# Chunk preparation of a gated DeltaNet: the decay matrix from matmuls, or from cumulative sums read back by DMA

## The chip, the cores and the metric

The kernel runs on one core of one Trainium2 chip. The time is device microseconds of one execution. Three runs of the kernel before gave 1589.02, 1593.64 and 1592.56 us, so the median is 1592.56 us. The profile is of a further execution, which took 1596.21 us.

## The reference

One layer (DEPTH is 1) works on 1024 latent tokens and 256 context tokens of width 1024, all in float32. An input projection, fed by RMS norm and modulation, feeds two groups: a gated DeltaNet with 4 heads of 128 and a neighbourhood attention with 8 heads of 64. An output projection and a SwiGLU feed-forward layer (width 2816) follow. What matters here is the DeltaNet, which is scanned forward and backward over the 1280 tokens in chunks:

```
qkv = short_conv(p[..., :3 * DN_WIDTH], conv_w)          # centred, 5 taps, SiLU
g   = -exp(A_log) * softplus(a + dt_bias);  beta = sigmoid(b)
gam = cumsum(g) inside a chunk
decay = exp(where(tril, gam[:, None] - gam[None, :], -inf))
m   = where(strict, (k * beta) @ k.T * decay, 0);  a_mat = I + m
u, w: triangular solves with a_mat;   qk = where(tril, q @ k.T * decay, 0)
scan over the chunks: v_new = u - w S;  o = q exp(gam) S + qk v_new;  S = S exp(g_last) + k_dec.T v_new
```

For each chunk and direction the kernel needs the decay matrix (the exponential of differences of cumulative sums, zero on the wrong side of the diagonal), the masked product of the keys times that matrix, and the inverse of a_mat. All of this can be done before the scan begins.

## The kernel before, in words

**Tiling.** The kernel works with chunks of 128 tokens: NCH = 10 chunks (2 of context, 8 of latent tokens), 2 directions, 4 heads. That makes 20 preparations, each for the four heads of one chunk and direction, in tiles of 128 partitions by 4 x 128 float32 (256 KB).

**Order of the work.** All engines' instruction streams are written by one Python program, and each engine runs its own stream in that order. The projection is a list `jobs` (line 952): blocks of 128 output columns (`Block`: k, q, v of the DeltaNet, nk, nq of the attention) and wide pieces (`Wide`: z and nv). The loop of line 974 does job n's matmuls (`j.mm`, line 389, three split products of float32r at a time; `wide`, line 572), steps background generators between them (`bg.step`), evacuates the bank (`evac`), and then does the norm of job n - 1 and the `finish` of job n - 2 (transposes and products of k with k and q with k).

**The convolution.** For q and v blocks `evac` copies the bank into a tile `cr` and puts the whole convolution on VectorE behind it at the end of the job: for each of the two segments (context, latent) one multiplication (line 441) and four multiply-adds (line 445), so ten instructions for v and five for q; `silu` (line 452, ScalarE) follows directly.

**The background.** `bg` holds two generators. `block_inverses` makes the decay tables (`decay_tables`, line 711: G, the cumulative exponentials EG, KD, ET) and then the inverses of the 32 x 32 diagonal blocks. Its end (lines 841 to 847) transposes the blocks and stores both forms in HBM as `x_d`. `preps` (line 853) makes the 20 preparations: at most three are alive at a time, each steps in turn, and a preparation takes seven steps. The four context preparations can run early; the 16 latent ones wait until the q blocks are finished (line 935). From then on `bg.step(3)` stands behind each of the eight row groups of a block, and `bg.step(5)` behind each tile of a wide piece (lines 1007, 1013). `bg.drain()` (line 984) completes them ahead of the last job.

**One preparation** (`prep`, line 879), with its steps separated by `yield`:

1. GpSimd multiplies the two halves of g (GH, GL, a high and a low float32r part) by a triangular mask into `rg` (line 886, two instructions); ScalarE and GpSimd spread the loaded blocks `xc` into `fx` (line 891) and `y` (line 892).
2. TensorE makes the differences of cumulative sums by three matmuls into one bank: two of `rg` against a mask (line 896) and one that adds -1e30 on the wrong side (line 897). ScalarE takes the exponential from PSUM into `e` (line 900). VectorE multiplies `kk` by e and by -beta, head by head (line 902, four instructions), and for latent chunks `at` by e (line 905); `at` is stored.
3. TensorE multiplies by the diagonal inverses (line 911, four matmuls), ScalarE evacuates (line 913).
4. to 6. Three rounds of small matmuls (line 920), each evacuated by VectorE (line 921). The result `y` is stored two ticks later.

Loads of a preparation (`fetch`, line 868: `kk`, `xc` and for latent chunks `at`) and all stores are issued on the SP queue, in the order of the program. A fetch is issued when no other fetched chunk is waiting. Buffers: kk 4, xc 3, at 3, e 2, rg 2, y 6.

**Around it.** Weights of the next job are loaded on SP at the start of a job, cast on ScalarE (line 198) and their low half is made on GpSimd (lines 199, 565). The convolution's early blocks (k) use another path (line 431). Behind the projections come the scan together with the attention, the output projection and the feed-forward layer, which read `y_d` and `at_d` from HBM.

## Time and profile before

| What | Value |
|---|---|
| Median of three runs | 1592.56 us (1589.02 to 1593.64) |
| The profiled execution | 1596.21 us, span of its instructions 1594.4 us |
| Busy share of the span: TensorE, its weight loads, VectorE, ScalarE, GpSimd | 93%, 78%, 64%, 45%, 13% |
| Granted TensorE clock, mean | 0.979 |
| DMA, mean over the span | 173 GB/s |
| Context preparations | about 295 to 336 us |
| Latent preparations | about 427 to 570 us |
| Scan and attention | about 600 to 850 us |

The span is the time from the first instruction to the last; a run's time is 1.8 us longer. "Busy" of TensorE is a union of modelled spans: consecutive matmuls overlap in it, so the distance from one start to the next tells more than a duration. Rows of groups give the count, the busy time, the mean duration of one instruction, and the engine's idle time ahead of them with what ended it.

### The profile page before, as it was taken

The numbers are of one execution on the slowest core, as the hardware profiler recorded it, in microseconds if no ns is written. First come the engines' busy times: TensorE is split into PE (matmuls) and PEld (weight loads), VectorE is DVE, ScalarE is ACT, GpSimd is POOL, SyncE is SP. The second block draws the span as 40 slices with busy tenths as digits, with TensorE's granted clock in tenths as the row PEclk, the third lists the DMA queues.
The fourth block names the chain that finished last, engine by engine and source line by source line (L and its number), as shares of the span: only waits on it lengthen the run. The fifth ranks groups of instructions, "written<-read, shape, count | busy, mean of one in ns | idle before, by whom it ended". The sixth has DMA issues, their size and how long they took to land.

```text
span 1594.4 us, 23945 instructions
## 1 busy us (share of the span) xinstructions
PE 1489.2 (93%) x8594; PEld 1239.2 (78%) x8594; DVE 1019.4 (64%) x1934; ACT 711.0 (45%) x1348; POOL 206.2 (13%) x278
## 2 busy tenths in 40 slices
PE   3999999899989997998897999999999999999999
PEld 1689788678978776887775877888888888888887
DVE  5866678335365565778886558866665555689652
ACT  5343362754435335666663246333333333545441
POOL 2044610532254200000000000000000000000000
PEclk9999999999999999999998999999999999999999
DMA  9457123444446369999737710623333333798742
GB/s 369 122 187 226 57 80 133 168 128 145 163 145 212 110 176 297 278 272 279 242 101 250 245 40 27 198 101 111 100 116 108 113 107 105 229 376 296 254 152 86
DMA packets 211528, 275.23 MB, mean 173 GB/s; under 512 B 15952, under 2 KB 119888, under 8 KB 210384
## 3 DMA queue, kind: packets, MB, share of 16 engines
q1 hardware_dynamic: 210544, 273.06, 53.1%
q8 instruction: 68, 1.11, 0.3%
q10 hardware_dynamic: 864, 0.63, 0.1%
q14 instruction: 52, 0.43, 0.1%
HBM read 206.78 MB, written 71.04 MB: 174 GB/s over the span
## 4 chain that ended last, share of the span: by engine, by line
PE 74%; DVE 7%; DMA 7%; ACT 6%; issue 3%; POOL 2%; SPq 1%; ACTq 0%; DVEq 0%; POOLq 0%
PE ps L1218 26%; PE ps L1565 13%; PE blk L389 11%; PE blk L572 4%; PE ps L1349 4%; PE sc L317 2%; PE pr L920 2%; PE sc L307 2%; PE sc L295 1%; PE ps L1111 1%; DVE tt L824 1%; PE ps L1371 1%; DMA fraw<-w_conv 1%; PE pr L911 1%; PE ps L1128 1%
## 5 line engine op out<-in xcount | busy, mean ns | idle before, releaser
L389 PE MATMUL blk<-hh,whi 128*128 128x512 f32 (+1 forms) x416 | 127.3, 399 | 4.1 <-ACT whi L198 1.6
L389 PE MATMUL blk<-hh,wlo 128*128 128x512 f32 (+1 forms) x416 | 120.8, 385 | 2.3 <-POOL wlo L199 2.3
L1279 ACT CAST uhi<-ws 128x512 fp32r<-128x512 f32 x91 | 54.7, 623 | 150.8 <-PE ps L1218 76.4
L1279 ACT CAST uhi<-wq 128x512 fp32r<-128x512 f32 x101 | 60.6, 621 | 137.0 <-issue 61.3
L389 PE MATMUL blk<-hl,whi 128*128 128x512 f32 (+1 forms) x416 | 119.2, 380 | 0.0
L1280 DVE TENSOR_TENSOR ulo<-wq,uhi 128x512 fp32r<-128x512 f32 x101 | 67.6, 688 | 68.3 <-ACT uhi L1279 37.2
L1218 PE MATMUL ps<-hT,uhi 128*128 128x512 f32 x336 | 104.7, 393 | 3.1 <-ACT hT L1397 3.1
L1218 PE MATMUL ps<-hT,ulo 128*128 128x512 f32 x336 | 103.9, 390 | 0.0
L1218 PE MATMUL ps<-lT,uhi 128*128 128x512 f32 x336 | 103.9, 391 | 0.0
L389 PEld LDWEIGHTS blk<-hh,wlo 128*128 128x128 f32 x416 | 75.3, 197 | 19.2 <-POOL wlo L199 2.9
L1218 PE MATMUL ps<-hB,uhi 128*128 128x512 f32 x288 | 89.7, 392 | 0.0
L1218 PE MATMUL ps<-lB,uhi 128*128 128x512 f32 x288 | 89.2, 391 | 0.0
L1218 PE MATMUL ps<-hB,ulo 128*128 128x512 f32 x288 | 89.1, 390 | 0.0
L389 PEld LDWEIGHTS blk<-hh,whi 128*128 128x128 f32 x416 | 72.2, 197 | 20.3 <-issue 3.0
L572 PE MATMUL blk<-zhi,hh 128*128 128x264 f32 (+1 forms) x288 | 85.2, 296 | 0.4 <-ACT kk L534 0.4
L389 PEld LDWEIGHTS blk<-hl,whi 128*128 128x128 f32 x416 | 74.4, 194 | 14.1
L1280 DVE TENSOR_TENSOR ulo<-ws,uhi 128x512 fp32r<-128x512 f32 x91 | 60.8, 686 | 37.3 <-ACT uhi L1279 29.0
L572 PE MATMUL blk<-zhi,hl 128*128 128x264 f32 (+1 forms) x288 | 83.4, 290 | 0.0
L572 PE MATMUL blk<-zlo,hh 128*128 128x264 f32 (+1 forms) x288 | 82.7, 287 | 0.0
L1218 PEld LDWEIGHTS ps<-hT,uhi 128*128 128x128 f32 x336 | 63.4, 189 | 16.6 <-ACT hT L1397 3.5
L1218 PEld LDWEIGHTS ps<-hT,ulo 128*128 128x128 f32 x336 | 63.4, 189 | 13.2
L1218 PEld LDWEIGHTS ps<-lT,uhi 128*128 128x128 f32 x336 | 63.4, 189 | 13.2
(331 smaller groups left out, 3614.9 us busy)
## 6 DMA issues: line engine op xcount, KB each, us to landing
wq<-w_fo SPq DMA_DIRECT2D x99, 256.0 KB
wq<-w_gu SPq DMA_DIRECT2D x88, 256.0 KB
wad<-wa SPq DMA_DIRECT2D x64, 256.0 KB
bt<-rpb SPq DMA_DIRECT2D x64, 192.0 KB
t_d<-g SPq DMA_DIRECT2D x22, 512.0 KB
fr<-t_d SPq DMA_DIRECT2D x44, 256.0 KB
f_d<-g SPq DMA_DIRECT2D x33, 256.0 KB
fr<-f_d SPq DMA_DIRECT2D x33, 256.0 KB
```

The source lines that it names most:

```text
L295: pe.matmul(sc[:, u * 640 + n0:u * 640 + n1], q, ks[i], start=i == 0, stop=i == 1)
L307: pe.transpose(sc[:, u * 640 + j * 128:u * 640 + (j + 1) * 128], bt[:, j * 128:(j + 1) * 128], ident)
L317: pe.matmul(sc[u * ND:u * ND + ND, 1280:1408], vv, pt[:, j * 128:(j + 1) * 128], start=j == 0, stop=j == 4)
L389: pe.matmul(o, ww[:, k], xx[k][:, s], start=k == 0 and j == 0, stop=k == KT - 1 and j == end)
L572: pe.matmul(p[:, :c1 - c0], x[k][:, s], ww[:, k, c0:c1], start=k == 0 and j == 0, stop=k == KT - 1 and j == 2)
L824: dve.tensor_tensor(t, N[:P, :, 0:c, c:c + 1].to_broadcast([P, 4, c, w]), N[:P, :, c:c + 1, c + 1:32].to_broadcast([P, 4, c, w]), OP.mult)
L920: pe.matmul(p[q, h * 128:h * 128 + 32 * r], f[:, h, q], y[:, h, s], start=True, stop=True)
L1218: pe.matmul(o, w[wi][:, k], x[xi][:, k], start=first and k == 0 and j == 0, stop=k == n - 1 and j == 2, skip_group_check=True)
L1279: act.copy(hi, self.raw[key])
L1280: dve.tensor_tensor(lo, self.raw[key], hi.bitcast(F32), OP.subtract)
L1349: pe.matmul(o, w[wi][:, k], parts[xi][k][:, s], start=k == 0 and j == 0, stop=k == KT - 1 and j == 2)
L1565: pe.matmul(o[b], w[wi][:, b], F[xn, p][xi], start=n in (0, 1, 5) and p == 0 and j == 0, stop=p == NFB // 2 - 1 and j == 2, skip_group_che ...
```

## The change

Three things change in the preparation, and two in what feeds it.

- **Decay matrix.** `decay_tables` keeps the negated cumulative sums `GN` (partition = token), transposes them once on TensorE, and stores the sums as 80 rows of 128 in HBM (`g_d`); G is clamped from below at -110. `fetch` loads the four rows of a chunk into every partition of `e` (a read of 2 KB repeated for 128 partitions). GpSimd sets the wrong side of the diagonal to -1e30 with `affine_select` (in place of the two products into `rg`), and ScalarE makes the exponential with the partition's own -sum as bias, head by head (four instructions from SBUF in place of one from PSUM). The three matmuls and their masks `mr[4]` and `mneg` are gone.
- **Beta.** -beta (`NB`) is multiplied into the stored diagonal inverses (two VectorE products of 128 x 1280 in `block_inverses`), so that `kk` is multiplied by e in one VectorE instruction and not in four.
- **Loads.** Up to two fetched chunks wait ahead of the running ones. Buffers: kk 5, xc 4, at 4, e 4 (now filled by the load), y 4.
- **Convolution.** The ten (or five) VectorE instructions of a block become a generator `taps`, stepped during the next job: two per row group of a block, three per tile of a wide piece; `silu` comes at its end.
- One `yield` is added in `decay_tables`, so everything behind it in `bg` is one step later.

```diff
@@ -135,8 +135,7 @@
     for i, v in enumerate((EPS, -0.5 * math.log(64.0))):
         dve.memset(bias[:, i:i + 1], v)
     b_eps, b_naq = bias[:, 0:1], bias[:, 1:2]
-    mr = const("mr", [128, 5, 128], F32R)
-    mneg = const("mneg", [128, 2, 128], F32R)
+    mr = const("mr", [128, 4, 128], F32R)
 
     v_d = dram.tile([T, 512], F32, name="v_d", tag="v_d")
     k_d = dram.tile([T, 512], F32, name="k_d", tag="k_d")
@@ -153,6 +152,7 @@
     y_d = dram.tile([2, NCH, 128, 4, 128], F32, name="y_d", tag="y_d")
     at_d = dram.tile([2, 8, 128, 4, 128], F32, name="at_d", tag="at_d")
     x_d = dram.tile([128, 2, 2, NU, 32], F32, name="x_d", tag="x_d")
+    g_d = dram.tile([2 * NU, 128], F32, name="g_d", tag="g_d")
     x2_d = dram.tile([KT, 128, L], F32, name="x2_d", tag="x2_d")
     f_d = dram.tile([NFB, 2, 128, 512], F32, name="f_d", tag="f_d")
     t_d = dram.tile([NFB, 2, 128, 512], F32, name="t_d", tag="t_d")
@@ -173,6 +173,7 @@
     EG = const("EG", [128, 2, NCH, 4])
     KD = const("KD", [128, 2, NCH, 4])
     ET = const("ET", [128, 2, NCH, 4])
+    GN = const("GN", [128, 2, NCH, 4])
     act.activation(sc2, c2, AF.Silu)
     bg = Background()
 
@@ -435,16 +436,24 @@
                 raw = cp.tile([128, T], F32, name="cr", tag="cr", bufs=2)
                 for p, s0, n in self.pss:
                     act.copy(raw[:, s0:s0 + n], p[:, :n])
+                self.later = self.taps(raw, acc, blk)
+
+            later = None
+
+            def taps(self, raw, acc, blk):
                 for lo, hi in ((0, CT), (CT, T)):
-                    if hi <= t0:
+                    if hi <= self.t0:
                         continue
                     dve.tensor_scalar(acc[:, lo:hi], raw[:, lo:hi], cw[:, blk, 2:3], None, op0=OP.mult)
+                    yield
                     for tap in (0, 1, 3, 4):
                         o = tap - 2
                         d0, d1 = max(lo, lo - o), min(hi, hi - o)
                         dve.scalar_tensor_tensor(acc[:, d0:d1], raw[:, d0 + o:d1 + o],
                                                  cw[:, blk, tap:tap + 1], acc[:, d0:d1],
                                                  op0=OP.mult, op1=OP.add)
+                        yield
+                self.silu()
 
             def silu(self):
                 acc, t0 = self.acc, self.t0
@@ -629,9 +638,6 @@
             wide = xp.tile([128, KT, 32], F32, name="wide", tag="wide")
             pool.memset(wide, 0.0)
             pool.tensor_copy(wide[:, :, 0:2], sc2)
-            pool.tensor_copy(mr[:, 4], ident)
-            for d in range(2):
-                pool.tensor_scalar(mneg[:, d], masks[:, d], -1.0e30, None, op0=OP.mult)
             pool.tensor_copy(mr[:, 0:4], masks)
             rs = xp.tile([128, T], F32, name="rs", tag="rs")
             acc = xp.tile([128, T], F32, name="acc", tag="acc")
@@ -736,6 +742,7 @@
             for d in range(2):
                 nb = nA[:, 4 * d:4 * d + 4].rearrange("p (o h) -> p o h", o=1).to_broadcast([128, NCH, 4])
                 dve.tensor_tensor(G[:, d], A[:, d], nb, OP.mult)
+            dve.tensor_scalar(G, G, -110.0, None, op0=OP.max)
             dve.tensor_scalar(B, B, 1.0, None, op0=OP.add)
             dve.reciprocal(B, B)
 
@@ -759,6 +766,13 @@
                     pe.matmul(pg[:, o:o + NU], m, g, start=True, stop=True)
             for q, t in enumerate((EG, KD, ET)):
                 act.activation(t.rearrange("p d c h -> p (d c h)"), pg[:, q * 2 * NU:(q + 1) * 2 * NU], AF.Exp)
+            gn = GN.rearrange("p d c h -> p (d c h)")
+            act.activation(gn, pg[:, :2 * NU], AF.Copy, scale=-1.0)
+            yield
+            p, rows = bank(), gp.tile([128, 128], F32, name="rows", tag="rows")
+            pe.transpose(p[:2 * NU, :128], gn, ident)
+            act.activation(rows[:2 * NU], p[:2 * NU, :128], AF.Copy, scale=-1.0)
+            sp.dma_start(g_d, rows[:2 * NU])
             yield
 
         def block_inverses():
@@ -842,8 +856,11 @@
                     ud = U[:, d * NU:(d + 1) * NU]
                     ut = g4.tile([128, NU, 32], F32, name="ut", tag="ut")
                     dve.transpose(fl(ut), fl(ud))
-                    sp.dma_start(x_d[:, d, d], ud)
-                    sp.dma_start(x_d[:, d, 1 - d], ut)
+                    x, s = (ut, ud) if d else (ud, ut)
+                    sp.dma_start(x_d[:, d, 0], x)
+                    dve.tensor_tensor(s, s, NB[:, d].rearrange("p c (h o) -> p (c h) o", o=1).to_broadcast(
+                        [128, NU, 32]), OP.mult)
+                    sp.dma_start(x_d[:, d, 1], s)
                     yield
 
         fl = lambda x: x.rearrange("p a b -> p (a b)")
@@ -861,46 +878,38 @@
                 def work(name, bufs=2, dt=F32):
                     return (pk if name == "kk" else pp).tile([128, 4, 128], dt, name=name, tag=name, bufs=bufs)
 
-                ys, fxs = [[work(f"{m}{i}", 1) for i in range(k)] for m, k in (("y", 6), ("fx", 2))]
+                ys, fxs = [[work(f"{m}{i}", 1) for i in range(k)] for m, k in (("y", 4), ("fx", 2))]
                 for t in ys + fxs:
                     pool.memset(t, 0.0)
 
                 def fetch(d, c):
 
-                    kk, xc = work("kk", 4), pp.tile([128, 2, 4, 32], F32, name="xc", tag="xc", bufs=3)
+                    kk, xc = work("kk", 5), pp.tile([128, 2, 4, 32], F32, name="xc", tag="xc", bufs=4)
+                    e = work("e", 4)
+                    u = (d * NCH + c) * 4
+                    sp.dma_start(fl(e), g_d[u:u + 4].rearrange("h t -> (h t)").partition_broadcast(128))
                     sp.dma_start(kk, kk_d[:, c])
                     sp.dma_start(xc, x_d[:, d, :, c * 4:c * 4 + 4])
                     at = None
                     if c >= 2:
-                        at = work("at", 3)
+                        at = work("at", 4)
                         sp.dma_start(at, qk_d[:, c - 2])
-                    return d, c, kk, xc, at
-
-                def prep(n, d, c, kk, xc, at):
+                    return d, c, kk, xc, e, at
+
+                def prep(n, d, c, kk, xc, e, at):
                     lat = c >= 2
-                    mle = M[C_LE + d].rearrange("p (o i) -> p o i", o=1).to_broadcast([128, 4, 128])
-                    rgs = []
-                    for gg in (GH, GL):
-                        rg = work("rg", 2, F32R)
-                        src = gg.bitcast(F32)[:, d, c].rearrange("p (h o) -> p h o", o=1).to_broadcast([128, 4, 128])
-                        pool.tensor_tensor(rg, src, mle, OP.mult)
-                        rgs.append(rg)
-                    y, fx = ys[n % 6], fxs[n % 2]
+
+                    pool.affine_select(e, e, pattern=[[0, 4], [1 - 2 * d, 128]], compare_op=OP.is_ge, fill=-1.0e30,
+                                       base=0, channel_multiplier=2 * d - 1)
+                    y, fx = ys[n % 4], fxs[n % 2]
                     for b in range(4):
                         q = slice(b * 32, b * 32 + 32)
                         act.copy(fx[q, :, q], xc[q, 1])
                         pool.tensor_copy(y[q, :, q], xc[q, 0])
                     yield 1
-                    p = bank("pr")
-                    for j, rg in enumerate(rgs):
-                        pe.matmul(p, mr[:, d], fl(rg), start=j == 0, stop=False)
-                    pe.matmul(p, mr[:, 4], mneg[:, d].rearrange("p (o i) -> p o i", o=1).to_broadcast([128, 4, 128]),
-                              start=False, stop=True)
-                    e = work("e", 2)
-                    act.activation(fl(e), p, AF.Exp)
                     for h in range(4):
-                        dve.scalar_tensor_tensor(kk[:, h], kk[:, h], NB[:, d, c, h:h + 1], e[:, h],
-                                                 op0=OP.mult, op1=OP.mult)
+                        act.activation(e[:, h], e[:, h], AF.Exp, bias=GN[:, d, c, h:h + 1])
+                    dve.tensor_tensor(kk, kk, e, OP.mult)
                     if lat:
                         dve.tensor_tensor(at, at, e, OP.mult)
                         stores.append((at_d[d, c - 2], at, tick[0] + 2))
@@ -932,7 +941,7 @@
                 live, landing = [], []
                 n = 0
                 while live or todo or landing:
-                    if not landing and todo and (todo[0][1] < 2 or all(x in done for x in queries)):
+                    while len(landing) < 2 and todo and (todo[0][1] < 2 or all(x in done for x in queries)):
                         landing.append(fetch(*todo.pop(0)))
                     if landing and len(live) < 3:
                         live.append(prep(n, *landing.pop(0)))
@@ -990,9 +999,12 @@
             fin = blk(n - 2) if n - 2 not in done else None
             fin = fin.finish() if fin else iter(())
             nrm = blk(n - 1)
+            taps = nrm and nrm.later or iter(())
             if isinstance(j, Wide):
                 for t, _ in enumerate(j.tiles()):
                     next(fin, 0)
+                    for _ in range(3):
+                        next(taps, 0)
                     if t == 4 and nrm:
                         nrm.norm()
                         for _ in fin:
@@ -1008,6 +1020,8 @@
             elif j:
                 for k in range(KT):
                     j.mm([k])
+                    next(taps, 0)
+                    next(taps, 0)
                     if k >= 3:
                         next(fin, 0)
                     bg.step(1 if n < turn else 3)
@@ -1023,7 +1037,7 @@
                         sp.dma_start(vw_d[:, cb, ch], vlat[4 * ch:4 * ch + 4, BLKS[cb]:BLKS[cb] + 32])
             if nrm:
                 nrm.norm()
-            if isinstance(j, Block):
+            if isinstance(j, Block) and j.later is None:
                 j.silu()
 
         dve.tensor_scalar(SQ, SQ, EPS, None, op0=OP.add)
```

## The prediction

> **What bounds the kernel now.** I read the page first, then busy times by stage, then TensorE's waits and its starts inside the stage of the change. From the page, engines and the chain that ended last:
>
> ```profile
> PE 1489.2 (93%) x8594; PEld 1239.2 (78%) x8594; DVE 1019.4 (64%) x1934; ACT 711.0 (45%) x1348; POOL 206.2 (13%) x278
> ...
> PE 74%; DVE 7%; DMA 7%; ACT 6%; issue 3%; POOL 2%; SPq 1%; ACTq 0%; DVEq 0%; POOLq 0%
> ```
>
> TensorE holds 74% of the chain. The stages (context preparations in the second row, latent ones in the third, scan and everything after it in the last):
>
> ```profile
> core 0: us, PE busy (x) PEld busy (x) DVE busy (x) ACT busy (x) POOL busy (x), PEclk, DMA share, GB/s
> ...
> 290.00:345.00 55.00, 47.85 (x262) 35.03 (x263) 19.01 (x34) 35.66 (x61) 28.96 (x57) 0.97 0.45 140
> 345.00:430.00 85.00, 84.64 (x521) 75.18 (x520) 37.30 (x45) 40.02 (x56) 15.64 (x8) 0.98 0.43 138
> 430.00:600.00 170.00, 157.42 (x1126) 128.21 (x1125) 102.93 (x185) 69.60 (x132) 61.72 (x82) 0.98 0.54 165
> 600.00:1594.40 994.40, 952.13 (x5216) 792.01 (x5215) 663.70 (x1418) 442.81 (x901) 19.53 (x60) 0.99 0.56 179
> ```
>
> Between 430 and 600 us TensorE is busy for 157.4 of 170 us and no other engine for more than 103, so matmuls taken out of this stage shorten it, and so do TensorE's waits. Between 345 and 430 there are no preparations and no waits to speak of: only the convolutions of q move there, and they cannot matter. Behind 600 us nothing is changed.
>
> **The change, part by part.** *Three matmuls fewer.* The busy column overstates them, because consecutive matmuls overlap in it; what counts is from start to start (timeline of TensorE, two preparations):
>
> ```profile
> 437.39 0.70 PE L896 MATMUL pr<-rg,mr 128*128 128x512 f32 x2 [0.73 <-ACT kk L913]
> 437.93 0.39 PE L897 MATMUL pr<-mneg,mr 128*128 128x512 f32 x1
> 438.16 0.63 PE L389 MATMUL blk<-hh,wlo 128*128 128x512 f32 x2
> ...
> 452.18 0.63 PE L896 MATMUL pr<-rg,mr 128*128 128x512 f32 x2
> 452.65 0.40 PE L897 MATMUL pr<-mneg,mr 128*128 128x512 f32 x1
> 452.88 0.28 PE L572 MATMUL blk<-zhi,hh 128*128 128x256 f32 x1
> ```
>
> The three take 438.16 - 437.39 = 0.77 and 452.88 - 452.18 = 0.70 us; I take 0.73. Sixteen latent preparations give 16 x 0.73 = 11.7 us, all of it on the path. The four context ones (2.9 us) run where TensorE also waits for others; I count half, 1.5. Together **-13.2 us** (bounds 16 x 0.70 = 11.2 and 20 x 0.77 = 15.4). The one added transpose and its two small evacuations are under a microsecond once, beside projection matmuls.
>
> *Waits of TensorE.* Groups in 430 to 600 us:
>
> ```profile
> L911 PE MATMUL pr<-fx,kk 128*128 128x96 f32 x128 | 21.2, 281 | 8.8 <-DVE kk L902 5.7 <-issue 3.1
> ```
>
> These 8.8 us are the most of the 12.6 that TensorE stands idle in the stage. The largest, with what VectorE did then and how TensorE ran behind it (two timelines):
>
> ```profile
> 460.65 0.28 PE L572 MATMUL blk<-zhi,hl 128*128 128x256 f32 x1
> 460.77 0.28 PE L572 MATMUL blk<-zlo,hh 128*128 128x256 f32 x1
> 464.88 0.74 PE L911 MATMUL pr<-fx,kk 128*128 128x96 f32 x2 [3.83 <-DVE kk L902]
> ...
> 465.69 0.41 PE L572 MATMUL blk<-zhi,hl 128*128 128x256 f32 x1
> 465.90 0.41 PE L572 MATMUL blk<-zlo,hh 128*128 128x256 f32 x1
> ```
> ```profile
> 457.66 4.83 DVE L445 SCALAR_TENSOR_TENSOR cacc<-cr,cw,cacc 128x255 f32<-128x255 f32 x4
> 462.40 2.42 DVE L902 SCALAR_TENSOR_TENSOR kk<-kk,NB,e 128x128 f32<-128x128 f32 x1
> ```
>
> The product kk by e stood behind 4.83 us of convolution, and its first head then took 2.42. The next largest is the same thing one block later:
>
> ```profile
> 532.20 3.62 DVE L445 SCALAR_TENSOR_TENSOR cacc<-cr,cw,cacc 128x254 f32<-128x254 f32 x2
> ```
> ```profile
> 536.19 0.43 PE L911 MATMUL pr<-fx,kk 128*128 128x96 f32 x2 [2.80 <-issue]
> ```
>
> With the taps spread over the next job and kk done by one instruction, such a burst cannot stand ahead of kk. I take **-7** of the 8.8 us (bounds 0 and -8.8).
>
> *Clock.* Behind the 3.83 us wait the same matmuls go 465.90 - 465.69 = 0.21 us apart, where they went 0.12 before it.
>
> ```profile
> 300.00:320.00 20.00, 14.13 (x94) 9.91 (x93) 7.35 (x18) 17.55 (x33) 12.92 (x30) 1.00 0.32 98
> ...
> 460.00:480.00 20.00, 16.17 (x121) 14.96 (x120) 12.07 (x18) 8.07 (x14) 9.68 (x9) 0.83 0.31 87
> ```
>
> 20 us at a clock of 0.83 lose 20 x 0.17 = 3.4 us. Without that wait I take **-3** (bounds 0 and -3.4). The Trainium skill (TensorE: Matmul & The Clock Gate, Part 1: The HAM clock gate) states that an idle window of about 3.4 us drops the clock to half until a busy window has passed; the trace agrees in kind, with 3.83 us of wait and the 0.21 us behind it. By that rule alone the shorter waits cost no clock and the 3.4 us come back whole, 0.4 more than I take.
>
> One rule of the Trainium skill (Perfetto Trace Analysis, Identifying the Most-Contended Engine) speaks against reading 93% as a full engine: matmul busy time misleads, and the share of the weight loads is the better measure. Here that is 128.21 / 170 = 75%, so by the rule the stage has 25% or 42 us of slack, and fewer matmuls alone might not shorten it; by busy time it has 12.6 us. The starts above, 0.23 us apart per matmul without a gap, side with busy time.
>
> *The other engines' new work.* Groups of the whole span:
>
> ```profile
> L445 DVE SCALAR_TENSOR_TENSOR cacc<-cr,cw,cacc 128x1022 f32<-128x1022 f32 (+3 forms) x48 | 56.7, 1195 | 0.9
> ...
> L199 POOL TENSOR_TENSOR wlo<-wraw,whi 128x1024 fp32r<-128x1024 f32 x18 | 44.3, 2459 | 186.4 <-ACT whi L198 179.9 <-issue 6.4
> ...
> L902 DVE SCALAR_TENSOR_TENSOR kk<-kk,NB,e 128x128 f32<-128x128 f32 x80 | 32.9, 465 | 23.9 <-ACT e L900 23.6
> ...
> L886 POOL TENSOR_TENSOR rg<-GH,cst 128x512 fp32r<-128x512 f32 x20 | 22.6, 1132 | 46.3 <-PE pr L896 46.1
> ...
> L900 ACT ACTIVATE e<-pr 128x512 f32<-128x512 f32 x20 | 11.9, 596 | 9.5 <-PE pr L897 9.4
> L905 DVE TENSOR_TENSOR at<-at,e 128x512 f32<-128x512 f32 x16 | 11.3, 703 | 0.0
> L1149 ACT ACTIVATE sq<-oacc 128x128 f32<-128x128 f32 x32 | 9.5, 298 | 2.2 <-DVE oacc L1124 2.2
> ```
>
> VectorE: 4 x 0.465 = 1.86 us become one product like L905, 0.70: 1.16 less per preparation. ScalarE: 0.60 becomes 4 x 0.298 = 1.19: 0.6 more per preparation, 12 us in all, beside TensorE's matmuls where ScalarE has 100 of 170 us free; from 300 to 320 us it has not (17.55 of 20). GpSimd: two instructions of rg, 1.13 each by this row, go. The trace has no affine_select; the nearest rows for 128 x 512 are the memset below (0.53) and half of L199 (1.23). I take 1.1, as for rg. Even at twice 1.23 GpSimd is no busier than now, and it runs ahead of TensorE, up to the four buffers of e. The chain from a preparation's start to L911 becomes shorter: no matmul stands in it any more.
>
> ```profile
> L866 POOL MEMSET y<- x6: 516/528/539, 291.1 to 293.4; 128x512 f32 x6
> ```
>
> DMA: 20 loads of e, each of the size of one kk load:
>
> ```profile
> kk<-kk_d SPq DMA_DIRECT2D x20, 256.0 KB
> ```
>
> In 430 to 600 us 165 GB/s x 170 us = 28.05 MB took 0.54 x 170 = 91.8 us of the queues, so 256 KB take about 0.86 us, and 16 of them 13.7: hidden, with the share going from 0.54 to (91.8 + 13.7) / 151 = 0.70. SP issues them ahead of kk; behind them in its queue wait xc, at, the stores and the weights' loads. If the cover is gone, POOL's mask is late first, then ScalarE's exponential, then what stands behind it there (L913 and the evacuations). y with 4 buffers makes GpSimd's copies wait for a store of four preparations ago; they are needed three rounds later. For these new waits together (a kk product behind two or three taps of 1.2 us, an exponential behind a late mask) I add **+2 us** (bounds 0 and 8.8, the waits that stand there today).
>
> *Context preparations.* Two products of 128 x 1280 enter VectorE ahead of the last stores of x_d:
>
> ```profile
> L802 DVE TENSOR_TENSOR W<-W,NB 128x1280 f32<-128x1280 f32 x1 | 3.6, 3573 | 8.0 <-ACT W L797 8.0
> ...
> L804 DVE TENSOR_TENSOR W<-W,cst 128x1280 f32<-128x1280 f32 x1 | 1.5, 1492 | 0.0
> ```
>
> The same broadcast took 3.57 (L802) and another 1.49: 3.0 to 7.1 us later for the second direction, plus one step. TensorE is then in projection matmuls until the first context product wants its data (waits from 290 to 430 us):
>
> ```profile
> PE pr L911 <- DVE kk L902: 2.7, 2, 2.2
> PE pr L920 <- ACT kk L913: 2.0, 1, 2.0
> ```
>
> I add **+2 us** (bounds -4.7, both of these waits gone, and +7.1).
>
> **Sum**: -13.2 - 7 - 3 + 2 + 2 = -19.2 us. The profiled execution's 1596.2 (span 1594.4 and 1.8 around it) becomes 1577.0. It stood 3.6 above the median of 1592.6, so beside the runs shown I forecast 1573.4, **1573 us**.
>
> **Rivals.** *A: only the matmuls count.* The taps still take VectorE as long, and during a block two of them (2.4 us) stand ahead of each row group's products, so the waits come back as many small ones and the clock still dips: -13.2 + 4 (new waits and contexts) = 1583. For it: L445's 56.7 us stay. Against: TensorE's large waits all stood behind bursts.
>
> *B: everything gives.* All 8.8 and 3.4 us, the 4.7 of the contexts, and 15.4 of matmuls: -32, 1560. For it: the chain ahead of L911 loses a TensorE pass. Against: ScalarE is full just where the contexts run.
>
> *C: slower, through the repeated read.* Place: the loads of e, 128 times the same 2 KB. If one holds the queues for T instead of 0.86 us, the stage needs 91.8 + 16 T of DMA; it decides from (151 - 91.8) / 16 = 3.7 us on, and the kernel is slower than before from (170 - 91.8) / 16 = 4.9 us on. At 5.5: 179.8, 9.8 over the present stage, 1602. For it: no load of this kind and size is in the trace. Against: size and packets are kk's.
>
> *D: it doesn't pass on.* The stage ends sooner, but scan and attention wait for their first loads all the same: 1592. Against: those are issued behind the last y store and would move with it.
>
> **Chances.** Forecast 0.58, A 0.17, B 0.10, C 0.08, D 0.07. The forecast's own range is 1564 to 1582. The range 1560 to 1587 takes in A and B and leaves out C and D. A measurement here can tell about 0.3% (4.8 us) from no change. Faster: the first three, 0.85. Within 0.3%: D and a little of A, 0.08. Slower: C, 0.07.
>
> **What would show it.** The first attention matmul, at 596.6 us in the trace of before, comes some 19 us sooner and everything behind it lasts as long as now. TensorE's wait ahead of the product of step 3 falls from 8.8 to under 3 us, and no 20 us slice of the latent stage has a clock of 0.83. Masks on GpSimd take about 1.1 us, exponentials 0.3 each. I am wrong if GpSimd waits for e's load and ScalarE for GpSimd in most preparations (C), if VectorE is the releaser of many short waits (A), or if the scan starts no earlier (D).

## The result, and the profile after

The changed kernel took 1567.17 us (median of four runs, 1560.74 to 1570.02) beside 1593.1 us for the kernel before (four runs, 1589.02 to 1595.03): a ratio of 0.9838, 95% interval 0.9818 to 0.9858, which is 25.9 us less. A second set of runs beside the experiments gave 1564.06 us and 0.9809 (0.9793 to 0.9824). The forecast was 1573 and its range 1560 to 1587. The profiled execution took 1570.02 us, 26.2 less than the one of before.

The page of the kernel after, busy time by engine:

```profile
PE 1473.0 (94%) x8535; PEld 1228.2 (78%) x8535; DVE 1000.3 (64%) x1877; ACT 721.1 (46%) x1406; POOL 185.6 (12%) x253
```

The same stages as in the prediction, now of the kernel after; the third row is 20 us shorter, since the stage has become some 20 us shorter:

```profile
core 0: us, PE busy (x) PEld busy (x) DVE busy (x) ACT busy (x) POOL busy (x), PEclk, DMA share, GB/s
290.00:345.00 55.00, 53.27 (x294) 39.41 (x293) 22.93 (x30) 45.46 (x90) 25.19 (x45) 1.00 0.64 207
345.00:430.00 85.00, 80.82 (x510) 72.58 (x509) 34.16 (x43) 38.06 (x59) 18.00 (x11) 0.96 0.47 148
430.00:580.00 150.00, 140.66 (x1057) 117.65 (x1058) 90.12 (x143) 76.85 (x166) 46.05 (x69) 0.97 0.70 212
580.00:1568.20 988.20, 953.98 (x5216) 793.22 (x5215) 661.34 (x1408) 440.45 (x896) 19.76 (x60) 0.98 0.55 179
```

Where the time went is read from one mark, the first attention matmul (timelines of TensorE, before and after):

```profile
596.58 0.27 PE L295 MATMUL sc<-kh,qs 128*128 128x256 f16 x1 [0.78 <-ACT cr L477]
```
```profile
573.29 0.27 PE L296 MATMUL sc<-kh,qs 128*128 128x256 f16 x1 [0.78 <-ACT cr L486]
```

It comes 23.3 us sooner; the other 2.9 of the 26.2 us come behind it. Of the 23.3, only 2.1 are there when the first v block starts (425.3 before, 423.2 after), so 21 us belong to the latent stage. What has become of the preparation's instructions there (groups of the kernel after; the page's usual columns):

```profile
L908 POOL COPY y<-xc 32x128 f32<-32x128 f32 x80 | 35.5, 443 | 31.4 <-DMA y_d<-y 13.8 <-PE pr L929 8.0 <-DMA xc<-x_d 6.4
L902 POOL TENSOR_SCALAR_AFFINE_SELECT e<-e 128x512 f32<-128x512 f32 x20 | 14.7, 733 | 28.1 <-DMA e<-g_d 25.0 <-DVE kk L912 2.6
L911 ACT ACTIVATE e<-e,GN 128x128 f32<-128x128 f32 x80 | 26.8, 393 | 13.3 <-POOL e L902 13.0
L912 DVE TENSOR_TENSOR kk<-kk,e 128x512 f32<-128x512 f32 x20 | 15.3, 765 | 11.4 <-ACT e L911 7.6 <-issue 1.5 <-POOL e L902 1.4
L920 PE MATMUL pr<-fx,kk 128*128 128x96 f32 x120 | 16.8, 285 | 0.0
```

The last row is that of the latent stage alone: the 8.8 us that TensorE waited there are gone. But a wait of the next step is new, and the clock dips as before, 20 us earlier in the trace (TensorE's waits from 253 to 600 us; its timeline; the clock in slices of 20 and of 4 us):

```profile
PE pr L929 <- ACT kk L922: 3.5, 2, 3.0
```
```profile
449.77 0.28 PE L581 MATMUL blk<-zlo,hh 128*128 128x256 f32 x1
453.08 0.64 PE L929 MATMUL pr<-y,kk 128*32 128x32 f32 x8 [3.03 <-ACT kk L922]
```
```profile
440.00:460.00 20.00, 16.97 (x125) 15.45 (x125) 14.74 (x18) 9.25 (x26) 13.67 (x17) 0.83 0.73 226
...
452.00:456.00 4.00, 2.92 (x19) 2.86 (x20) 3.48 (x4) 2.54 (x8) 3.80 (x6) 0.58 0.80 254
456.00:460.00 4.00, 4.00 (x27) 3.78 (x27) 0.67 (x1) 2.65 (x10) 1.81 (x2) 0.57 0.33 101
```

Who is late there is seen on GpSimd and ScalarE (two timelines):

```profile
448.13 3.33 POOL L200 TENSOR_TENSOR wlo<-wraw,whi 128x1024 fp32r<-128x1024 f32 x1 [2.03 <-ACT whi L199]
451.40 0.82 POOL L902 TENSOR_SCALAR_AFFINE_SELECT e<-e 128x512 f32<-128x512 f32 x1
```
```profile
452.26 0.40 ACT L911 ACTIVATE e<-e,GN 128x128 f32<-128x128 f32 x1 [3.40 <-POOL e L902]
452.57 0.46 ACT L922 COPY kk<-pr 128x384 f32<-128x384 f32 x1
```

The mask stood behind a low half of the weights, the exponential behind the mask, and behind the exponential ScalarE's evacuation that TensorE wanted. It is the order that the prediction named for the case that GpSimd's cover is gone.

A second new wait lies ahead of the latent stage, where the prediction expected nothing ("they cannot matter"). TensorE comes to the squares of q at 357.3 us, some 7 us sooner than before, but ScalarE finishes them only some 4 us sooner. TensorE waits for 3.4 us, and the slice behind it has a lower clock than before (TensorE's waits from 253 to 600 us after; the slice before and after):

```profile
PE m L479 <- ACT cr L464: 3.4, 1, 3.4
```
```profile
360.00:380.00 20.00, 19.64 (x96) 16.33 (x95) 11.13 (x10) 10.01 (x13) 5.08 (x2) 0.91 0.46 150
```
```profile
360.00:380.00 20.00, 19.34 (x95) 17.02 (x96) 6.80 (x8) 7.51 (x11) 4.75 (x2) 0.83 0.49 164
```

### The profile page after: what moved, and what is told of

Read it like the earlier page. It is cut to its first block, busy times and chain, and to the rows that moved or that the text cites. A ratio compares the mean times of both kernels' runs of the same rounds, so it can differ in the third digit from the quotient of the medians.

```text
span 1568.2 us, 23886 instructions
## 1 busy us (share of the span) xinstructions
PE 1473.0 (94%) x8535; PEld 1228.2 (78%) x8535; DVE 1000.3 (64%) x1877; ACT 721.1 (46%) x1406; POOL 185.6 (12%) x253
## 4 chain that ended last, share of the span: by engine, by line
PE 67%; ACT 4%; DMA 4%; DVE 3%; issue 2%; POOL 1%; SPq 1%; DVEq 0%; POOLq 0%; ACTq 0%
PE ps L1232 27%; PE ps L1579 13%; PE blk L390 6%; PE ps L1363 4%; PE blk L581 3%; PE sc L318 2%; PE sc L308 2%; PE sc L296 2%; PE pr L929 2%; PE ps L1125 1%; PE ps L1385 1%; PE pr L920 1%; PE ps L1137 1%; PE ps L1142 1%; PE ps L1106 1%
## 5 line engine op out<-in xcount | busy, mean ns | idle before, releaser
L1232 PEld LDWEIGHTS ps<-hT,ulo 128*128 128x128 f32 x336 | 63.2, 188 | 13.2
```

What stands on the lines that cost most here:

```text
L1232: pe.matmul(o, w[wi][:, k], x[xi][:, k], start=first and k == 0 and j == 0, stop=k == n - 1 and j == 2, skip_group_check=True)
```

## The experiments

Each was timed beside the kernel before on the same chip. "Mark" is the start of the first attention matmul in the profile, "behind" the time from there to the start of the last matmul.

| Kernel | Ratio to before (95%) | Median, us | Mark, us | Behind, us |
|---|---|---|---|---|
| before | 1 | 1593.83 (beside the first four) | 596.6 | 993.6 |
| after, again | 0.9809 (0.9793 to 0.9824) | 1564.06 | 572.8 | 982.9 |
| before, taps spread | 1.0002 (0.9992 to 1.0012) | 1594.30 | 597.5 | 995.9 |
| after, taps in a burst | 0.9828 (0.9811 to 0.9844) | 1567.47 | 574.6 | 990.2 |
| after, three idle matmuls | 0.9894 (0.9882 to 0.9907) | 1577.51 | 581.1 | 992.7 |
| after, beta taken back | 0.9814 (0.9793 to 0.9836) | 1565.83 | 574.6 | 987.5 |
| before, beta moved | 0.9967 (0.9950 to 0.9984) | 1588.78 | 594.0 | 990.2 |
| after, one fetch ahead | 0.9802 (0.9784 to 0.9820) | 1562.76 | 568.7 | 986.2 |
| after, low halves on VectorE | 0.9796 (0.9778 to 0.9813) | 1561.67 | 568.8 | 985.8 |
| decays alone | 0.9825 (0.9797 to 0.9853) | 1564.59 | 571.5 | 987.2 |
| after, a small TensorE pass | 0.9919 (0.9896 to 0.9941) | 1579.48 | 581.4 | 991.9 |
| after, one fetch and low halves | 0.9803 (0.9777 to 0.9829) | 1561.06 | 567.1 | 989.5 |
| after, loads of e twice | 0.9964 (0.9951 to 0.9976) | 1587.72 | 590.6 | 988.5 |

**The kernel after, again.** Nothing is edited.

> The changed kernel once more, beside the others on one chip. All theories: 25 to 27 us below the kernel before (ratio 0.983 to 0.985). What it adds is the time behind the first attention matmul: between that matmul and the last one the kernel before took 993.6 us and the changed one 990.7 in their first profiles. If that difference is noise, this profile lies between 989 and 995 without a pattern; if the change did something behind the projections, it lies at 990 to 991 again, and the runs that keep the old convolution go back to 993.6.

The ratio lies below the expected 0.983 to 0.985. The mark agrees with the first profile to 0.5 us; the time behind it was 982.9, below both expectations. By this one pair, the marks of two profiles can be compared to a microsecond or so, and the time behind them to some 8. Nearly all of these 8 us are clock: behind the mark the stretches at half the clock add up to 30.7 us in the first profile and 17.1 in the second, which loses 15.4 and 8.5 us.

**The taps, alone and taken back.** The one kernel is before with

```
-                for tap in ...: dve.scalar_tensor_tensor(...)     # all in evac
+                self.later = self.taps(raw, acc, blk)             # stepped in the next job
```

and the other is after with the same lines put back.

> The kernel before, with the convolution alone spread over the next job (two taps per row group, three per tile). My theory: TensorE's wait ahead of the step-3 product falls from 8.8 us to under 3 and the 20 us slice at clock 0.83 around 460 us goes: 7 + 3 = 10 us below the kernel before, ratio 0.992 to 0.995. Rival A (only the matmuls count; the waits come back as many small ones behind taps): 0 to 2 us below, ratio 0.999 to 1.000, the wait ahead of the step-3 product still 6 us or more.

> The changed kernel, with the convolution put back as one burst at a block's end and the activation behind it. My theory: the waits and the dip come back, 7 to 10 us above the changed kernel, 16 to 19 below the kernel before, ratio 0.988 to 0.990; TensorE's wait ahead of the step-3 product is 6 us or more again. A rival: one VectorE product in place of four is what emptied that wait, and the burst costs nothing: ratio 0.983 to 0.985, the wait under 3 us. Rival A: 0.983 to 0.985 too, but with the wait back and no time lost.

Spread alone, the taps gained nothing (1.0002), the slice from 460 to 480 us still has a clock of 0.83, and the wait that they were to remove is still there (groups of that kernel, 430 to 600 us):

```profile
L919 PE MATMUL pr<-fx,kk 128*128 128x96 f32 x128 | 21.2, 287 | 7.9 <-DVE kk L910 4.9 <-issue 2.8
```

Taken back from the changed kernel they cost 1.8 us at the mark, 3 in the median with intervals that overlap, and the wait stays away, against the theory of either run:

```profile
L912 PE MATMUL pr<-fx,kk 128*128 128x96 f32 x119 | 16.5, 284 | 0.8 <-DVE y L922 0.8
```

The reason is seen in the kernel before, in rows that stand right behind those of the prediction (timeline of VectorE):

```profile
464.75 1.30 DVE L445 SCALAR_TENSOR_TENSOR cacc<-cr,cw,cacc 128x1023 f32<-128x1023 f32 x1
465.98 0.37 DVE L902 SCALAR_TENSOR_TENSOR kk<-kk,NB,e 128x128 f32<-128x128 f32 x1
466.27 1.34 DVE L445 SCALAR_TENSOR_TENSOR cacc<-cr,cw,cacc 128x1022 f32<-128x1022 f32 x1
```

The program writes the ten taps in one loop, yet a product of a preparation that is written later stands between two of them. The description of the kernel above says that each engine runs its stream in the order of the program. That is not so: the framework evidently plans the order anew. Side by side, the changed kernel and the one with the burst have the same 1877 instructions on VectorE, and only five of them stand elsewhere. The edit of the taps asked for an order that the planner was largely making already.

**The matmuls.** After, with a use of TensorE that nobody waits for:

```
                     yield 1
+                    p = bank("pr")
+                    for i in range(3):
+                        pe.matmul(p, mr[:, d], mr[:, 0:4] as 128x512, start=i == 0, stop=i == 2)
```

> The changed kernel, with three 128x512 matmuls into a bank of their own put back into each preparation, at the place where they stood; nobody reads their result. My theory: TensorE's time is the bound, 20 x 0.73 = 14.6 us above the changed kernel (13 to 16), ratio 0.992 to 0.994. The rival by the weight loads' share (a stage with 42 us of slack): under 5 us above, ratio 0.983 to 0.987, the first attention matmul moved by less than 5 us from 573.3.

The ratios differ by 0.0085, 13.5 us (9 to 18 by the ends of their intervals), where 14.6 were expected; the mark moved by 8.3 (572.8 to 581.1). Up to the first v block nothing is lost (its start came at 420.7, against 422.1 without the matmuls), from there to the mark 160.4 us are needed in place of 150.7. So matmul time counts in the latent stage, 9.7 us for 16 preparations. It is free for the four context ones: there it shortens the wait for the squares of q, from 3.1 to 1.4 us. In the new wait's place (440 to 460 us) the clock is now 0.99: the new wait is not there in that kernel. A shorter one stands ahead of it (1.9 us at 436), and the clock loses 1.7 us between the first v block and the mark, where it lost 3.4 without the matmuls; so their own time is rather 11 us than 9.7. Behind the mark, where nothing was edited, lies the rest of the 13.5. By the rule of the Trainium skill that goes by the share of weight loads (Perfetto Trace Analysis, Identifying the Most-Contended Engine), this stage had 42 us of slack in the kernel before and the matmuls should have cost little; 9.7 us for 16 preparations say otherwise.

**Beta, taken back and alone.** In the one the two products of `block_inverses` go and four come back per preparation; in the other the reverse is done to the kernel before:

```
-                    dve.tensor_tensor(kk, kk, e, OP.mult)
+                    for h in range(4):
+                        dve.scalar_tensor_tensor(kk[:, h], kk[:, h], NB[:, d, c, h:h + 1], e[:, h], ...)
```

> The changed kernel with beta taken back: x_d as in the kernel before, kk multiplied by e and -beta head by head in four VectorE instructions. Half of what the change gained in the latent stage is no matmul time, and the spread convolution alone gained nothing, so two theories are left for it. M (the single product cannot be cut up by taps between its heads and takes 1.2 us less): the wait ahead of the step-3 product is back at 4 to 8 us, the first attention matmul at 577 to 582, ratio 0.985 to 0.988. S (the chain of a preparation is shorter without a TensorE pass and the mask and exponential run ahead): the wait stays under 3 us, first attention matmul at 572 to 575.5, ratio 0.981 to 0.983.

> The kernel before with beta alone moved into the inverses: one product kk by e in place of four. M: the waits ahead of the step-3 product fall from 12.3 us (290 to 600 us) to under 6, the first attention matmul comes at 587 to 592 in place of 596.6, ratio 0.994 to 0.997. S: the wait stays above 8 us, since e still comes out of a TensorE bank behind a projection job, first attention matmul at 594 to 597, ratio 0.998 to 1.001.

Taken back, beta costs 1.8 us at the mark and leaves the wait away (0.4 us for the product): M falls. Alone it gains 4.8 us (0.9967) and 2.6 at the mark: the ratio is that of M, the mark that of S. The waits that VectorE's product ends are as they were, 8.4 us before and 8.3 now; 3.9 us more, which the trace of before puts to no releaser, are gone (TensorE's waits of that kernel from 290 to 600 us):

```profile
PE pr L912 <- DVE kk L904: 8.3, 6, 3.7
```

**The decays alone.** After, with burst, four products and one fetch ahead; left are the loads of e, mask, exponentials, and the buffers.

> The changed kernel with three of its parts taken back: the convolution in one burst, beta in four VectorE instructions, one fetched chunk ahead. Left of the change are the decays by DMA, mask and exponential (and the sizes of the buffers). Theory S (the decays alone make the gain: no matmul time and no TensorE pass in the chain): first attention matmul at 568 to 576, ratio 0.980 to 0.984. A rival (the parts only look free one at a time, since each covers for the other): first attention matmul past 578, ratio above 0.986.

Mark 571.5, ratio 0.9825: all of the gain within the uncertainty. The parts do not cover for one another; the decays are the change, together with the deeper buffers. No run has the decays by DMA with the buffers of before (e 2, kk 4), so what the buffers add is not known.

**A small pass.** After, with

```
+                    p, gb = bank("pr"), pp.tile([128, 4], ...)
+                    pe.matmul(p[:, :4], ident, GN[:, d, c], start=True, stop=True)
+                    act.copy(gb, p[:, :4])
                     for h in range(4):
-                        act.activation(e[:, h], e[:, h], AF.Exp, bias=GN[:, d, c, h:h + 1])
+                        act.activation(e[:, h], e[:, h], AF.Exp, bias=gb[:, h:h + 1])
```

> The changed kernel with a small TensorE pass put back into the chain: at the place of the three matmuls one matmul of 128x4 carries the negated sums into a bank, ScalarE copies them out, and the four exponentials take them from there. It costs TensorE some 2 us in all. Theory S1 (the gain beside the matmul time comes from the pass itself, which makes e wait behind the projection's matmuls and a bank): the wait ahead of the step-3 product comes back, TensorE's waits from 430 us to the first attention matmul grow by 5 us or more, that matmul comes at 579 to 587, ratio 0.985 to 0.990. Theory S2 (it comes from GpSimd: one mask of 0.73 us in place of two products of 1.13, so that VectorE's products beside it run undisturbed, and from VectorE): the pass costs its own 2 us and little more, first attention matmul at 573 to 577, ratio 0.981 to 0.983.

Mark 581.4, ratio 0.9919: 8.6 us at the mark, where the 20 matmuls take 3.4 us from start to start. The ratios are 17 us apart; the other half lies behind the mark, where nothing was edited, and takes the ratio past that of S1, too. The wait is back (TensorE's waits of that kernel, 290 to 600 us; its stages):

```profile
PE pr L923 <- DVE kk L915: 6.5, 5, 2.3
```
```profile
290.00:345.00 55.00, 47.67 (x266) 34.71 (x265) 17.18 (x24) 43.05 (x81) 20.14 (x37) 0.97 0.56 180
```

So S1 holds, by the mark and the wait. What the pass does is told by when the products kk by e run: three windows of that line alone, for the kernel before, after, and after with the pass (the columns here are busy VectorE with its count, clock, DMA share and GB/s):

```profile
290.00:345.00 55.00, 7.05 (x16) 0.97 0.45 140
345.00:430.00 85.00, 0.20 (x1) 0.98 0.43 138
430.00:600.00 170.00, 25.68 (x64) 0.98 0.54 165
```
```profile
290.00:345.00 55.00, 4.96 (x7) 1.00 0.64 207
345.00:430.00 85.00, 0.69 (x1) 0.96 0.47 148
430.00:580.00 150.00, 9.65 (x12) 0.97 0.70 212
```
```profile
290.00:345.00 55.00, 2.77 (x4) 0.97 0.56 180
345.00:430.00 85.00, 0.00 (x0) 1.00 0.51 159
430.00:590.00 160.00, 13.14 (x16) 0.98 0.63 197
```

With the pass, and in the kernel before, none but the context preparations (4 instructions, or 16 at four each) has its product before 430 us, but for one head. In the changed kernel eight have: the four contexts and four latent ones, these at 330 to 347 us, though the program starts a latent preparation only when the q blocks are finished. The product needs nothing of q, and nothing of TensorE any more; so it runs when its loads are there. From the end of the last product of a preparation to the start of its first matmul (each from the timelines, median of the 16 latent ones) it is -0.7 us before (the first head's matmul starts before the last head is done), 0.3 us with the pass, and 13.9 us in the changed kernel, never under 8. The kernel with three idle matmuls is the control: it has the matmul time without the dependence, eight products before 430 us, and a lead of 24.1 us. With such a lead, neither taps nor four products can make TensorE wait, and that is why both parts looked free. Which part of the pass takes the lead away (the place in TensorE's queue, the bank or ScalarE's copy) the run does not separate.

**One fetch ahead.**

```
-                    while len(landing) < 2 and todo and (...):
+                    if not landing and todo and (...):
```

> The changed kernel with one fetched chunk ahead in place of two, the buffers as they are. My theory: a load takes 2 to 3 us to land and a preparation some 8, so one ahead is early enough: first attention matmul within 1.5 us of 573, ratio 0.980 to 0.983. A rival (the masks' cover is the second load ahead): GpSimd waits for e's loads over 50 us in place of 25, TensorE's waits behind the mask grow by 3 us or more, first attention matmul past 576, ratio 0.983 to 0.986.

The second load ahead does nothing for the time that these runs resolve (0.9802), and in the profile the mark is 4.1 us sooner without it, more than expected. The premise was off, too: in the changed kernel the masks that wait for their load start 4.5 us or more behind its issue, not 2 to 3. GpSimd waits less for e (18.7 us from 290 to 600 us, 25.0 with two ahead), the 3.0 us wait is gone, and with it the dip:

```profile
440.00:460.00 20.00, 18.68 (x158) 16.68 (x158) 15.12 (x23) 10.58 (x30) 11.46 (x17) 1.00 0.80 237
```

Why the mask's place in the queue is better then was not tried; the planner makes another order.

**Low halves on VectorE, and both.**

```
-                self.w = load_w(src, raw=raw)
+                lo = dve if self.kind == "v" or (self.kind, i) == ("nq", 3) else pool
+                self.w = load_w(src, raw=raw, lo_engine=lo)
```

> The changed kernel with the low half of the weights of the v blocks and of the last block made on VectorE (as in the later stages, 1.22 us) and not on GpSimd (2.4 to 3.3 us). The one long wait left in the latent stage (3.0 us at 450 us, with a 20 us slice at clock 0.83 behind it) stands behind a mask that is queued behind such a low half. My theory: with it off GpSimd's queue that wait and the slice's clock go, 3 to 6 us below the changed kernel: first attention matmul at 567 to 570, ratio 0.977 to 0.979. A rival (the low half is needed by TensorE in time, and on VectorE it stands behind taps and products): a new wait of the projection's matmuls for the low half takes its place, 0 to 3 us above the changed kernel.

> The changed kernel with one fetched chunk ahead and the low half of the v blocks' and the last block's weights on VectorE, each of which alone brought the first attention matmul from 573 to 569 in its profile. If they remove the same wait: 568 to 569 again, ratio 0.979 to 0.980. If they add up: 564 to 566, ratio 0.976 to 0.978. Time from the first attention matmul to the last one 983 to 991 us, as in the others with the decays by DMA.

The first brought the mark to 568.8 as expected, and the ratio to 0.9796, just above the expected range, but not by its reason: a wait of 2.2 us of the same kind is still there at 449 us, behind another order. Both together leave no such wait over 0.4 us and bring the mark to 567.1, in place of 573 and between the two expectations; in the time, 1561.06 us and 0.9803 cannot be told from the changed kernel's 0.9809. If it is a better kernel, it is by less than these runs resolve.

**Loads of e twice.**

```
+                    e2 = work("e2", 1)
+                    sp.dma_start(fl(e2), g_d[u:u + 4] to all partitions)
                     sp.dma_start(fl(e), g_d[u:u + 4] to all partitions)
-                        at = work("at", 4)
+                        at = work("at", 3)
```

> The changed kernel with every load of e made twice, the first time into a tile that nobody reads (one buffer; at has 3 buffers in place of 4 to make room): 20 more repeated reads of 2 KB into 128 partitions, 256 KB each. My theory (such a read takes the queues as long as any 256 KB, 0.86 us, and lies beside other work): the DMA share of 430 to 580 us goes from 0.70 to about 0.79, the first attention matmul within 2 us of 573, ratio 0.980 to 0.984. Rival C (a repeated read holds the queues for several us): at 3 us each the share would be at 1 and the first attention matmul past 590, ratio above 0.990.

It lost some 24 us (0.9964 against 0.9809), and not by either reason. The DMA share of the latent stage is 0.68 from 430 to 590 us, no more than before the edit, and this stage is no longer (147.3 us from the first v block to the mark, 150.7 without). The loss lies ahead of it, 253 to 443 us. Since nothing depends on the idle reads, the planner put all 20 of them there, and as they have one buffer, each waits on SP for the one before (SP's waits, 290 to 600 us):

```profile
SPq L891 <- DMA e<-g_d: 34.1, 10, 5.6
```

Behind them in SP's queue stood the weights, kk, and the k tiles. TensorE then waited 5.5 us for kTh, and 6.8 in place of 3.1 to 3.4 for the squares of q. The run shows what a waiting load costs on SP; it does not price the read itself. That price is had from the stages: 212 GB/s x 150 us = 31.8 MB took 0.70 x 150 = 105 us in the changed kernel, 0.87 us for 256 KB, against 0.86 before. In that mixture 12 loads of e are a tenth of the bytes, so a read of 3.7 us each, rival C's point, would have shown as 34 us more.

## Why the prediction was right, and where it was not

The direction, the range and the place (ahead of the first attention matmul) were right. Of the five terms, the matmuls and the waits had about the right size, the waits for a wrong reason; the new waits were somewhat larger, the clock's gain did not come, and the contexts had the wrong sign. That the misses of these last three (1.5, 3 and -4 us) nearly cancel is luck. The sum was 7 us short, 4 of them at the mark.

- **Matmuls, -13.2.** Measured 9.7 in the latent stage where 11.7 were put, or some 11 with the clock's share. The half for the contexts (1.5) comes to nothing at the first v block. The 13.5 between the ratios is nearer to the term by luck, since it takes in time behind the mark.
- **Waits, -7.** The 8.8 us are gone to 0.0 us, but the step that explains them failed: "With the taps spread over the next job and kk done by one instruction, such a burst cannot stand ahead of kk." Spreading changes nothing and one instruction little; what counts is that e no longer passes through TensorE's queue. The prediction had the sentence ("no matmul stands in it any more") and gave it to rival B, with 0.10, in place of counting it. The trace of before had the hint too: a product between two taps, against the order of the program.
- **Clock, -3.** Measured nothing: the slice with 0.83 moved from 460 to 440 us, behind the new 3.03 us wait, and the slice from 360 to 380 us fell from 0.91 to 0.83. From 290 us to the mark the stretches at half the clock lose 6.8 us before and 6.8 after. That "no 20 us slice of the latent stage has a clock of 0.83" was wrong.
- **New waits, +2.** Measured 3.5 us (L929) in the latent stage, of the kind that the prediction named: mask late, then exponential, then the evacuation. The 3.4 us for the squares of q (L479) come to it, in the stretch of which the prediction said that nothing there can matter.
- **Contexts, +2.** Wrong sign: the first v block starts 2.1 us sooner, and TensorE is busy for 53.3 of the 55 us from 290 to 345, where it was for 47.9. The pass puts 47.7 back; the two products of 1280 lay beside projection matmuls. The gain there is larger than what is left of it: at 290 us the changed kernel is 4 us behind, at 357 us some 7 ahead, and the wait for the squares of q with the clock behind it takes 5 back.
- **Prices.** Masks 0.73 us (1.1 put), exponentials 0.39 (0.30), kk 0.77 (0.70), the DMA share 0.70 as worked out. They lie off the path while the lead is 8 us or more, except where something urgent stands behind them in the same queue, as at 449 us. That GpSimd would be "no busier than now" at twice 1.23 was a slip (2.46 against 2.26 us); at 0.73 it does not matter.
- **Mark and what is behind.** What was to come "some 19 us sooner" came 23.3 and 23.8 us sooner. Behind it the prediction had nothing; the runs have 25.9 and 29.8 in all. The time behind the mark was 990.2 to 995.9 us in five profiles with a TensorE pass or idle matmuls in the preparation, and 982.9 to 990.7 in the nine others: 5 us between the means, with an overlap at 990. Nothing was edited there. Much of the scatter is clock: without what the stretches at half the clock lose, the five need 975.7 to 980.0 us and the nine 973.8 to 976.5, 3 us between the means. What makes these 3 us stays open.

Of the rivals, A fell (no small waits came back), C by the unchanged price per byte, D by the mark. B had the mechanism, and its 1560 is as near to the 1564 to 1567 measured as the forecast's 1573; but it counted the clock's 3.4 us too, which did not come.

By the marks, the change in the latent stage and ahead of it is made up so: 594.0 - 596.6 = -2.6 from beta; 581.1 - 594.0 = -12.9 from decays that no longer wait for TensorE (GpSimd's and ScalarE's changed work, the fetches and the taps in it); 572.8 - 581.1 = -8.3 from the matmuls' own time. These are differences of single profiles, and the clock alone shifts each by 1.7 or 3.4 us; the order of size holds, not the tenths.

## What to carry to other kernels

Before pricing a matmul that helps to prepare an operand, ask whose queue it ties the preparation to: moving it off the bounding engine can be worth more than its own time, since everything ahead of it may then run as soon as its loads land. Measure the lead of an operand over its use; while it is several microseconds, the number and order of the small instructions that make it matter little, except to what stands behind them in their engines' queues. An engine that gets ahead in one stage may only wait in the next, so ask which operand it will want then. Where a framework plans the order, read each engine's order from the trace, not from the program, and give a small price to an edit that only rewrites the order; idle work without dependents, added as a probe, is moved too.

## What the hardware showed beyond that

- Waits shorter than expected cost clock. Behind 3.03 us of wait the granted clock was 0.58 and 0.57 in the next two slices of 4 us, a loss of 8 x 0.42 = 3.4 us, about as much again as the wait. The Trainium skill (TensorE: Matmul & The Clock Gate, Part 1: The HAM clock gate) puts the drop behind an idle window of about 3.4 us; here 3.03 us was enough, and with the low halves on VectorE a wait of 2.2 us went with 0.85 and 0.72 in two slices, as these rows of that kernel show:

```profile
448.00:452.00 4.00, 2.20 (x19) 2.16 (x20) 1.85 (x3) 2.89 (x9) 2.39 (x6) 0.85 0.82 274
452.00:456.00 4.00, 4.00 (x35) 3.82 (x35) 2.04 (x4) 2.98 (x11) 0.11 (x1) 0.72 0.66 229
```

- The clock goes down in fixed portions. In these traces it is either full or one half, and every half, but for one cut off at the end of each trace, lasts 3.41 us or two or three times that: 6.83 us from 452.64 on in the kernel after (a window laid on them shows 0.50), 3.41 us from 450.83 on with the low halves on VectorE. So 0.91 and 0.83 in a slice of 20 us are one and two such portions, 1.7 and 3.4 us lost.

- GpSimd's mask of 128x512 takes 0.64 us as a rule and 1.59 at most, near the memset (0.53) and not near a product (1.1 to 1.2), as the row of its durations in the kernel after says (least, median and greatest in ns, first and last start):

```profile
L902 POOL TENSOR_SCALAR_AFFINE_SELECT e<-e x20: 636/637/1586, 303.5 to 513.9; 128x512 f32<-128x512 f32 x20
```

- A read that repeats 2 KB of HBM into 128 partitions moves its 256 KB at the price of any other load, as far as the stage's share of 0.70 at 212 GB/s can show it.
